# One encoder layer on one core: eight modulation dots moved into the feed-forward's first product, and a block of half 1 summed on chip

## The chip, the cores and the metric

The kernel runs on one core of a Trainium2 chip. The metric is the device time of one execution in microseconds (us), as the median of several executions. One core has a matrix engine (TensorE, PE in the profile; its weight loads are PEld), an elementwise engine (VectorE, DVE), an activation engine (ScalarE, ACT), a general engine (GpSimd, POOL) and an engine that mostly issues DMAs (SyncE, SP). Each runs its own instructions in its own order and waits on semaphores for the others.

## The reference

One layer on x of 1024 positions by 1024 features, in fp32, with one conditioning vector c:

```python
mod = silu(c) @ w_ada + b_ada                 # 6 x 1024 numbers
sh1, sc1, gt1, sh2, sc2, gt2 = split(mod, 6)
h = rmsnorm(x, norm1_g) * (1 + sc1) + sh1
u, v, q, k, va, gate_a, gate_b = split(h @ w_in)
a_out = gmlp_branch(u, v, ...) @ w_a          # spatial gating over chunks of 128
b_out = window_attention_branch(q, k, va, ...) @ w_b
merged = sigmoid(gate_a) * a_out + sigmoid(gate_b) * b_out
x = x + gt1 * (merged @ w_o)
h2 = rmsnorm(x, norm2_g) * (1 + sc2) + sh2
f_gate, f_up = split(h2 @ w_ffn_in)           # 2 x 2816
x = x + gt2 * ((silu(f_gate) * f_up) @ w_ffn_out)
```

## The kernel before

**Products.** Activations lie transposed: features in the 128 partitions, positions along the row. A product of fp32 numbers is made of three products of rounded parts (`mm3`): each operand is split into a high part (a CAST on ACT: `wh`) and the rest (a subtraction on DVE: `wl`), and high times high, high times low and low times high go into one PSUM bank. So every 128 x 1024 unit of weights costs a DMA into a `raw` tile, one CAST on ACT and one subtraction on DVE (a few on POOL) before PE may use it. Nearly all operations are issued through helpers that record every instruction, so almost all rows of the profile carry line 76 (L76); tile names tell them apart.

**Stages.** The 1024 positions are worked in two halves of 512, `hf` 0 and 1. For each half: the QKV products; the attention in eight steps of scores, exponentials, `normalise`, transposes and values, with pieces of other products put in as fillers; the gMLP products; and the branch products `d` = 0..7. In half 1 these are followed by the two sigmoid gates of both halves, by w_o for half 0 (d = 0..7) and for half 1, then by the feed-forward's first product in 22 rows `f` of seven products each (`product(f, i)`, with its evictions in `evict(f, i)`), then by its second product.

**Block products.** The gates and the feed-forward multiply 2 x 2 blocks with seven instead of eight products. The activations' blocks for the gates are made in `block_sums`, from four chunks per k = 0..3: `a0`, `a1` (normalised and scaled x of half 0, from DRAM `x0d`) and `b0`, `b1` (half 1, from DRAM `x1sd`, loaded by POOL's DMA queue in `block_load`). From them come B11, B21 (half 0 plus the shift SH1), T1 to T4 (differences and sums; b1 - b0, b0 - a0, and so on) and B22, which is half 1's second block plus shift, and which is there already as the two tiles `h` (high and low) of half 1's QKV input. `block_part` writes a block's high part by ACT and returns a function that writes the low part by DVE. The eight calls (k, part) are `jobs` at the branch steps d = 2k + part.

**Modulation dots (adaLN).** The first 16 columns of `mod` (SH1, SC1) are made at the start. The other 32 (GT1, SC2, SH2, GT2, eight each) wait in `ada_queue`; each is a dot of a 128 x 1024 tile of weights with `silu_c`, the broadcast silu(c), done by DVE as a multiply with accumulation. They come whole (`ada_load` and `ada_next`), as halves of 128 x 512 in two `hs` or `xs` tiles (`ada_half_load`, `ada_half`), or as pairs loaded by POOL's queue (`ada_pair_load`). Before, five are done in half 0's branch stage, four in half 1's QKV, five in half 1's attention, twelve in the gates, four in w_o of half 0 and two as halves in w_o of half 1. `silu_c` lies in a pool that the feed-forward takes over.

**What sets the order.** A scheduler orders the code of a stage by due times; where `in_order[0]` is set, and in the feed-forward (`tc.manual_schedule()`), the order is that of the code. SP and POOL issue DMAs in order, so a load that waits for a free tile holds up those behind it. `stream("hs")` and `stream("xs")` have two tiles each.

In half 1's attention the dots stand in the step itself, ahead of `normalise`:

```python
            if hf == 1 and 0 < s < 6:
                ada_half("hs" if s < 5 else None)
            elif hf == 1 and s == 0:
                ada_half_load()
            normalise(sc[0], sc[2], den)
```

Of the kernel before, what the change touches and what calls it, by code (L numbers as in the profile page):

```python
# [8 lines left out]
F32 = mybir.dt.float32  # L9
# [3 lines left out]
ALU = mybir.AluOpType  # L13
# [3 lines left out]
P = 128  # L17
# [21 lines left out]
def kernel(  # L39
# [73 lines left out]
    def stream(tag):  # L113
        return t2.tile([P, 512], F32, tag=tag, name=nm(tag), bufs=2)
# [120 lines left out]

    rows_d = lambda n, name, w=HALF: dram.tile([n, P, w], F32, tag=name, name=name)
    x0d, x1sd, pd = rows_d(KT, "x0d"), rows_d(KT, "x1sd"), rows_d(KT, "pd", 2048)
    md = [rows_d(KT, f"md{h}") for h in range(2)]

    apool_ctx = ExitStack()  # L240
# [336 lines left out]
        V.tensor_tensor(s, m[:, :, 0], m[:, :, 1], op=ALU.add)  # L577
        rstd(s, NT, rcol[1])

    dsh = const.tile([P, 16], F32, tag="dsh", name="dsh")[:, :4]  # L580
    blk = {}

    chunk = {}

    def block_load(k, name):
        if k < 4:
            chunk[name] = stream("hs" if name[0] == "a" else "xs")
            store(chunk[name], (x0d if name[0] == "a" else x1sd)[4 * int(name[1]) + k])

# [9 lines left out]
                                              op0=ALU.add, op1=ALU.subtract)  # L599

    def block_sums(k, part, kinds):
        c = slice(k, k + 1)
        a0, a1, b0, b1 = (chunk[x] for x in ("a0", "a1", "b0", "b1"))
        b11 = lambda: block_part("B11", k, a0, kinds[0], mod[:, SH1 + k : SH1 + k + 1])
        b21 = lambda: block_part("B21", k, a1, kinds[0], mod[:, SH1 + 4 + k : SH1 + 5 + k])
        t2 = lambda: block_part("T2", k, b1, kinds[1], mod[:, SH1 + 4 + k : SH1 + 5 + k])
        if k == 3 and part == 0:
            low = b11()
            V.tensor_tensor(b1, b1, b0, op=ALU.subtract)
            low1 = block_part("T3", k, b1, kinds[1], dsh[:, c])  # L610
            low()
            low2 = b21()
            low1()
            low2()
# [3 lines left out]
        if k == 3:  # L618
            V.tensor_tensor(b0, b0, a0, op=ALU.subtract)
            added(b1, a0)  # L620
            low = t2()
            V.tensor_tensor(a1, b1, a1, op=ALU.subtract)
            low1 = block_part("T4", k, a1, kinds[2])
            low()
            low = block_part("T1", k, b0, kinds[1])
            low1()
            low()
            return
        if part == 0:
            if k == 0:  # L630
                V.tensor_tensor(dsh, mod[:, SH1 + 4 : SH1 + 8], mod[:, SH1 : SH1 + 4], op=ALU.subtract)
            V.tensor_tensor(b1, b1, b0, op=ALU.subtract)
            low3 = block_part("T3", k, b1, kinds[1], dsh[:, c])
            V.tensor_tensor(b0, b0, a0, op=ALU.subtract)
            low1 = block_part("T1", k, b0, kinds[1])
            low3()
            added(b1, a0)
            low2 = t2()
            low1()
            low2()  # L640
            block_load(k + 1, "b0")
            for x in blk["B22"]:
                A.activation(x[:, k, :], x[:, k, :].bitcast(F32), AF.Copy, scale=-1.0)
            return
        low, low1 = b11(), b21()
        low()
        low1()
        block_load(k + 1, "a0")
        V.tensor_tensor(a1, b1, a1, op=ALU.subtract)
        low = block_part("T4", k, a1, kinds[2])  # L650
        block_load(k + 1, "b1")
        low()
        block_load(k + 1, "a1")
# [86 lines left out]
    def half(hf):  # L740
# [319 lines left out]
        for s in range(nw):  # L1060
            if s:
                prepare_due()
                sc = q_step(s)
                pts = transposed(st)
                den = exps(*sc, work[s][1])
            fill(FA)
            if hf == 0 and 0 < s < 7:
                x_square(s + 1)
            if hf == 0 and s == 7:
                x_rstd()  # L1070
            if hf == 1 and 0 < s < 6:
                ada_half("hs" if s < 5 else None)
            elif hf == 1 and s == 0:
                ada_half_load()
            normalise(sc[0], sc[2], den)
            if s == 0:
                end_unit()
            st = sc[0]
            if s == nw - 1:
                for vg in vgs:  # L1080
                    act[0] = after(A.activation(vg, vg, AF.Gelu_apprx_tanh), act[0])
                for t, vg in enumerate(vgs[:3]):
                    V.tensor_tensor_reduce(
                        out=stream("hs"), in0=vg, in1=vg, op0=ALU.mult, op1=ALU.add,
                        scale=1.0, scalar=0.0, accum_out=vr[:, t : t + 1])
# [81 lines left out]
        for d in range(KT):  # L1167
            in_order[0] = d < 2
            if 0 < d < KT - 1:
                wab.append(unit(None, V, abr.pop(0)))  # L1170
                if d + 2 + hf < KT:
                    abr.append(raw_unit(w_ab[d + 2 + hf]))
            elif d:
                if hf == 0:
                    early.append(unit(None, V, early_raw[0]))
                else:
                    gate_sums(2)
                    for low in gate_prep_b(2):
                        low()
            if hf and d == 5:  # L1180
                gate_load(2)
            if hf and d == 6:
                gate_prep_a(2)
            ms = []
            for br, t in ((1, (oH, oL)), (0, (gH, gL))):
                if hf and d == KT - 1 and br == 0:
                    held.append((wab[d], t))
                    continue
                pb = mm_bank()
                for k in range(4):  # L1190
                    kc = slice(br * Q + k * P, br * Q + (k + 1) * P)
                    mm3(pb, (wab[d][0][:, kc], wab[d][1][:, kc]), (t[0][:, k, :], t[1][:, k, :]),
                        k == 0, k == 3)
                if d < 2:
                    sg = gates.pop(0)
                    V.scalar_tensor_tensor(out=sg, in0=sg, scalar=1.0, in1=pb, op0=ALU.add,
                                           op1=ALU.mult)
                    ms.append(sg)
                else:
                    c = tmp()  # L1200
                    A.copy(c, pb)
                    j = 2 * hf + br
# [134 lines left out]
    for hf in range(2):  # L1337
# [14 lines left out]
        for d in range(KT):  # L1352
# [34 lines left out]
            if hf == 0:  # L1387
# [17 lines left out]
        sums.append(ss)  # L1405
        if hf == 0:
            m = m1
    assert not ada_queue

    def fpt(name):  # L1410
        return jt(F32R, 4)
# [298 lines left out]
    def split_step(n):  # L1710
        if n < len(work):
# [4 lines left out]
                            for x in "hl"]  # L1716
            split2(raws[n], *ready[n])

    with tc.manual_schedule():
        U[4, 0], U[5, 0], U[0, 0], U[1, 0] = early  # L1720
        buf = mid.tile([P, 2048], F32, tag="mid", name=nm("ws"))
# [44 lines left out]
        for f, i in steps:  # L1766
# [13 lines left out]
                evict(f, i)  # L1780
            if (f, i) == (0, 5):
                evict(0, 6)
            if i == 6 or (f, i) == (0, 5):
                hidden_sums(f)
            elif f > 2:
                run_later(1)
# [174 lines left out]
```

## Time and profile before

| what | value |
|---|---|
| time, median of 3 runs | 1276.61 us (1276.09 to 1276.81) |
| the profiled execution's own time | 1273.99 us |
| its span in the trace | 1272.2 us |
| mean granted TensorE clock | 0.992 |
| busy share of the span | PE 97%, DVE 72%, ACT 45%, POOL 13% |
| DMA | 236.29 MB, mean 186 GB/s |

The span begins with the first and ends with the last instruction of the trace; 1.8 us of the profiled execution's time lie outside it. In the timeline a row gives start, duration, engine, operation, output<-inputs, how many alike follow one another, and in brackets how long the engine stood idle before it and what ended that. In the table of windows each stretch of time has the busy time of every engine with its number of instructions, then the granted clock (PEclk, 1.00 is full), the DMA engines' busy share, and GB/s.

### The profile page before, as it was taken

The page shows a single profiled execution, that of the slowest core. Times are in us where ns is not written, and L with a number is a line of the kernel's source. Part 1 is how long each engine was busy: PE and PEld are TensorE (multiplying, and loading weights), DVE is VectorE, ACT ScalarE, POOL GpSimd, SP SyncE. Part 2 cuts the span into 40 slices and gives each one's busy share as a digit, 9 for nine tenths or more (in the row PEclk, how much of TensorE's full clock was granted, in tenths as well). Part 3 has the DMA queues.
Part 4 walks back from the last instruction along what each step waited for, and adds up shares of the span by engine and source line. Part 5 has one row for each costly group of instructions (what it writes and reads, how often), then busy time and mean ns, then how long its engine had stood idle before and what let it go on. Part 6 is the DMA issues. An engine that isn't in the chain of part 4 may idle for free.

```text
span 1272.2 us, 15652 instructions
## 1 busy us (share of the span) xinstructions
PE 1232.7 (97%) x5634; PEld 1016.3 (80%) x5634; DVE 915.1 (72%) x1545; ACT 577.7 (45%) x938; POOL 170.5 (13%) x216
## 2 busy tenths in 40 slices
PE   6999999999997999999899999999999999999998
PEld 4888887887885788887788888888888887888887
DVE  8898884488887699865888766676666675455646
ACT  5567854366776333443445332333332334433341
POOL 1224320013331001221100000000100000010001
PEclk9999999999999999999999999999999999999999
DMA  9622179313256466677621443554645548896652
GB/s 372 235 100 97 37 240 321 118 55 116 87 177 220 141 215 229 235 245 251 222 110 50 176 171 133 198 185 179 231 150 181 199 165 318 295 329 187 192 167 100
DMA packets 78448, 236.29 MB, mean 186 GB/s; under 512 B 9377, under 2 KB 9377, under 8 KB 72354
## 3 DMA queue, kind: packets, MB, share of 16 engines
q1 hardware_dynamic: 57458, 147.20, 33.9%
q0 software_dynamic: 17456, 81.80, 18.1%
q10 hardware_dynamic: 3456, 6.29, 1.3%
q8 instruction: 44, 0.72, 0.2%
q14 instruction: 34, 0.28, 0.1%
HBM read 178.11 MB, written 57.15 MB: 185 GB/s over the span
## 4 chain that ended last, share of the span: by engine, by line
PE 52%; issue 16%; DVE 12%; DMA 12%; ACT 6%; POOL 1%; SPq 0%; ACTq 0%; POOLq 0%; DVEq 0%
PE at L76 29%; PE mm L76 23%; DVE mid L76 3%; DVE wl L76 2%; ACT wh L76 2%; DMA wo<-in_w_out_dram 1%; DMA raw<-in_w_o_dram 1%; DMA xs<-x1sd 1%; DVE lb L76 1%; DVE xs L76 1%; ACT lb L76 1%; DMA hs<-in_w_ada_dram 1%; DMA wS<-wo 1%; DMA xs<-in_xT_dram 1%; DMA mid<-in_w_ada_dram 1%
## 5 line engine op out<-in xcount | busy, mean ns | idle before, releaser
L76 DVE TENSOR_TENSOR wl<-raw,wh 128x1024 fp32r<-128x1024 f32 x141 | 171.9, 1221 | 94.1 <-ACT wh L76 92.8
L76 ACT CAST wh<-raw 128x1024 fp32r<-128x1024 f32 x155 | 162.4, 1052 | 151.4 <-PE mm L76 51.4
L76 PE MATMUL mm<-mid,wh 128*128 128x512 f32 x696 | 215.5, 390 | 1.6 <-ACT wh L76 1.2
L76 PEld LDWEIGHTS mm<-mid,wh 128*128 128x128 f32 x696 | 130.2, 188 | 30.9 <-ACT wh L76 1.6
L76 PE MATMUL at<-j,wh 128*128 128x512 f32 x464 | 142.9, 389 | 0.0
L76 PE MATMUL mm<-mid,wl 128*128 128x512 f32 x348 | 135.5, 390 | 0.8 <-DVE wl L76 0.6
L76 PE MATMUL mm<-wh,h 128*128 128x512 f32 x384 | 130.9, 403 | 2.2 <-ACT h L76 2.2
L76 PEld LDWEIGHTS at<-j,wh 128*128 128x128 f32 x464 | 87.0, 188 | 18.2 <-ACT xs L76 0.2
L76 PE MATMUL mm<-j,wh 128*128 128x512 f32 x288 | 90.8, 397 | 4.8 <-ACT wh L76 4.8
L76 PE MATMUL at<-h,wh 128*128 128x512 f32 x288 | 91.1, 398 | 3.1 <-ACT h L76 2.8
L76 DVE TENSOR_TENSOR wl<-ws,wh 128x1024 fp32r<-128x1024 f32 (+1 forms) x55 | 62.0, 1128 | 44.4 <-ACT wh L76 44.4
L76 PE MATMUL at<-j,wl 128*128 128x512 f32 x232 | 90.4, 390 | 0.2 <-DVE wl L76 0.2
L76 PEld LDWEIGHTS mm<-wh,h 128*128 128x128 f32 x384 | 72.5, 191 | 17.0 <-ACT h L76 3.1
L76 PE MATMUL mm<-h,wh 128*128 128x512 f32 x272 | 84.6, 392 | 0.0
L76 ACT CAST wh<-ws 128x1024 fp32r<-128x1024 f32 (+1 forms) x55 | 53.6, 974 | 58.8 <-DVE ws L76 42.1
L76 PE MATMUL mm<-wl,h 128*128 128x512 f32 x192 | 77.2, 402 | 2.4 <-DVE wl L76 2.4
L76 PEld LDWEIGHTS mm<-mid,wl 128*128 128x128 f32 x348 | 65.3, 188 | 15.1 <-DVE wl L76 1.0
L76 PEld LDWEIGHTS mm<-j,wh 128*128 128x128 f32 x288 | 54.9, 192 | 16.4 <-ACT wh L76 5.2
L76 PEld LDWEIGHTS at<-h,wh 128*128 128x128 f32 x288 | 54.9, 192 | 15.4 <-ACT h L76 3.2
L76 PEld LDWEIGHTS mm<-h,wh 128*128 128x128 f32 x272 | 50.6, 188 | 10.4
L76 DVE TENSOR_TENSOR ol<-raw,oh 128x1024 fp32r<-128x1024 f32 x30 | 36.7, 1224 | 30.2 <-ACT oh L76 30.0
L76 PE MATMUL mm<-j,wl 128*128 128x512 f32 x144 | 57.5, 399 | 0.9 <-DVE wl L76 0.9
(277 smaller groups left out, 2529.7 us busy)
## 6 DMA issues: line engine op xcount, KB each, us to landing
raw<-in_w_gate_dram SPq DMA_DIRECT2D x28, 512.0 KB, 5.1
tA<-hid POOLq DMA_DIRECT2D x11, 1024.0 KB, 5.2
tB<-hid POOLq DMA_DIRECT2D x11, 1024.0 KB, 4.9
wo<-in_w_out_dram POOLq DMA_DIRECT2D x22, 512.0 KB, 4.8
wS<-wo POOLq DMA_DIRECT2D x11, 1024.0 KB, 5.5
raw<-wS SPq DMA_DIRECT2D x44, 256.0 KB, 3.4
raw<-tB SPq DMA_DIRECT2D x44, 256.0 KB, 4.3
hs<-in_w_ada_dram SPq DMA_DIRECT2D x42, 256.0 KB, 3.6
```

Source lines behind the costliest of these rows:

```text
L76: ins = f(*args, **kw)
```

## The change

Eight dots (GT2) go into the feed-forward: `silu_c` is stored to DRAM near the start, read back into two `hs` tiles at row 6, and rows 7 to 14 do one dot each, in two halves, from weights loaded a row ahead. The five dots of half 1's attention, three of half 0's branch stage, and the two in w_o of half 1 are gone from there; w_o of half 0 does six instead of four, with a third pair load. In the block sums, `b1` is no longer loaded: POOL adds the two parts of B22 (so it has the shift in it), and the biases of T1 to T4 are changed to fit (`nsh` is minus the shift). `gate_sums(2)` moves from d = 7 to d = 6.

```diff
+    silu_d = dram.tile([P, D], F32, tag="silu_d", name="silu_d")
...
     def block_load(k, name):
         if k < 4:
+            if name == "b1":
+                chunk[name] = stream("xs")
+                G.tensor_tensor(chunk[name], *(x[:, k, :].bitcast(F32) for x in blk["B22"]), op=ALU.add)
+                return
...
-        t2 = lambda: block_part("T2", k, b1, kinds[1], mod[:, SH1 + 4 + k : SH1 + 5 + k])
...
+        if part == 0:
+            if k == 0:
+                V.tensor_scalar(nsh, mod[:, SH1 : SH1 + 8], -1.0, None, op0=ALU.mult)
...
             V.tensor_tensor(b1, b1, b0, op=ALU.subtract)
-            low1 = block_part("T3", k, b1, kinds[1], dsh[:, c])
+            low3 = block_part("T3", k, b1, kinds[1], col(nsh, k))
...
+            added(b1, a0)
+            low2 = block_part("T2", k, b1, kinds[1])
...
-        low = block_part("T4", k, a1, kinds[2])
+        low = block_part("T4", k, a1, kinds[2], col(nsh, 4 + k))
...
-            if hf == 1 and 0 < s < 6:
-                ada_half("hs" if s < 5 else None)
-            elif hf == 1 and s == 0:
-                ada_half_load()
+            if hf == 0 and s == 0:
+                store(silu_d, silu_c)
...
-                    gate_sums(2)
...
             if hf and d == 6:
                 gate_prep_a(2)
+                gate_sums(2)
...
-                ada_next(d < 4)
+                ada_next(d < 1)
...
-                if d < 2:
-                    ada_half(None if d else "hs")
...
-                if d in (0, 2):
+                if d in (0, 2, 4):
                     ada_pair_load()
-                if 0 < d < 5:
+                if 0 < d < 7:
                     ada_next(False)
-                if d == 7:
-                    ada_half_load()
...
+    def gain_dots(f, i):
+        if f == EARLY and i == 0:
+            again.extend(stream("hs") for _ in range(2))
+            for j in range(2):
+                dma(again[j], silu_d[:, j * 512 : (j + 1) * 512])
+        if not ada_queue:
+            return
+        if f >= EARLY and i == 5:
+            again[2:] = [tmp(), tmp()]
+            for j in range(2):
+                dma(again[2 + j], w_ada2[ada_queue[0][0] - GT1][:, j * 512 : (j + 1) * 512])
+        if f > EARLY and i in (3, 4):
+            j = int(i == 4)
...
+            V.scalar_tensor_tensor(out=again[2 + j], in0=again[2 + j], scalar=1.0, in1=again[j],
+                                   op0=ALU.mult, op1=ALU.mult,
+                                   accum_out=part if j else acc_mod[:, col : col + 1])
```

PE's order of instructions is the same in both kernels. On the other engines the change moves rows at three places.

On DVE, in a step of half 1's attention, this stands before, between the sink's exponentials (`es`) and the sum of the softmax (`den`) by which `normalise` scales the probabilities `lb`:

```order
L76 TENSOR_TENSOR es_2902<-rows,nmx_2881 128x4
L76 SCALAR_TENSOR_TENSOR hs_2864,acc_mod<-hs_2864,silu_c 128x512
L76 SCALAR_TENSOR_TENSOR hs_2865,part_2949<-hs_2865,silu_c 128x512
L76 TENSOR_TENSOR acc_mod<-acc_mod,part_2949 128x1
L76 SCALAR_TENSOR_TENSOR mod<-acc_mod,badap,cc 128x1
L76 TENSOR_TENSOR den_2931<-den_2931,es_2902 128x4
```

and this after the change, at the same place:

```order
L76 TENSOR_TENSOR es_2888<-rows,nmx_2867 128x4
L76 TENSOR_TENSOR den_2917<-den_2917,es_2888 128x4
L76 RECIPROCAL den_2917<-den_2917 128x4
L76 TENSOR_SCALAR lb_2871<-lb_2871,den_2917 128x384
L76 TENSOR_SCALAR lb_2876<-lb_2876,den_2917 128x384
```

The four rows of a dot are gone, in each of five steps.

On DVE, at the end of half 1's attention and of its gMLP product, `mid_2677<-at,cc,mid_2677` are the evictions of the spatial product and `xs_3802<-xs_3802,xs_3798` is b1 - b0 of the first block sum. Before:

```order
L76 TENSOR_TENSOR xs_3675<-at_3670,xs_3675 64x512
L76 SCALAR_TENSOR_TENSOR mid_2677<-at_3711,cc,mid_2677 128x4x64 x2
L76 SCALAR_TENSOR_TENSOR mid_2677<-at_3720,cc,mid_2677 128x4x64 x2
L76 SCALAR_TENSOR_TENSOR mid_2677<-at_3729,cc,mid_2677 128x4x64 x2
L76 SCALAR_TENSOR_TENSOR mid_2677<-at_3738,cc,mid_2677 128x4x64 x2
L76 TENSOR_TENSOR mid_2681<-at_3761,mid_2680 128x512
L76 TENSOR_TENSOR mid_2681<-at_3768,mid_2680 128x512
L76 TENSOR_TENSOR mid_2681<-at_3775,mid_2680 128x512
L76 TENSOR_TENSOR xs_3802<-xs_3802,xs_3798 128x512
```

After:

```order
L76 TENSOR_TENSOR xs_3620<-at_3615,xs_3620 64x512
L76 TENSOR_TENSOR xs_3747<-xs_3747,xs_3743 128x512
L76 SCALAR_TENSOR_TENSOR mid_2667<-at_3656,cc,mid_2667 128x4x64 x2
L76 SCALAR_TENSOR_TENSOR mid_2667<-at_3665,cc,mid_2667 128x4x64 x2
L76 SCALAR_TENSOR_TENSOR mid_2667<-at_3674,cc,mid_2667 128x4x64 x2
L76 SCALAR_TENSOR_TENSOR mid_2667<-at_3683,cc,mid_2667 128x4x64 x2
L76 TENSOR_TENSOR mid_2671<-at_3706,mid_2670 128x512
```

The subtraction b1 - b0 (now `xs_3747`) stands ahead of the evictions instead of behind them.

On POOL at the same place, `mid<-xs,mid` is the last split of the attention's output and `wl<-raw,wh` a split of weights. Before:

```order
L76 TENSOR_TENSOR mid_2679<-xs_3675,mid_2678 64x4x128
L140 DMA xs_3802<-x1sd 128x512
L76 TENSOR_TENSOR wl_3708<-raw_3705,wh_3707 128x1024
L76 TENSOR_TENSOR wl_3758<-raw_3755,wh_3757 128x1024
L140 DMA hs_3900<-x0d 128x512
```

After:

```order
L140 DMA xs_3743<-x1sd 128x512
L76 TENSOR_TENSOR mid_2669<-xs_3620,mid_2668 64x4x128
L76 TENSOR_TENSOR xs_3747<-h_1927,h_1928 128x512
L76 TENSOR_TENSOR wl_3653<-raw_3650,wh_3652 128x1024
L76 TENSOR_TENSOR wl_3703<-raw_3700,wh_3702 128x1024
```

Where a load was issued, POOL now adds the two parts itself, between the split it has just done and the two splits of weights.

More of the change, by code (lines that the diff above doesn't have):

```diff
@@ L578, in x_rstd @@
         rstd(s, NT, rcol[1])
-    dsh = const.tile([P, 16], F32, tag="dsh", name="dsh")[:, :4]
+    nsh = const.tile([P, 16], F32, tag="nsh", name="nsh")[:, :8]
     blk = {}
@@ L601, in block_sums @@
     def block_sums(k, part, kinds):
-        c = slice(k, k + 1)
         a0, a1, b0, b1 = (chunk[x] for x in ("a0", "a1", "b0", "b1"))
-        b11 = lambda: block_part("B11", k, a0, kinds[0], mod[:, SH1 + k : SH1 + k + 1])
-        b21 = lambda: block_part("B21", k, a1, kinds[0], mod[:, SH1 + 4 + k : SH1 + 5 + k])
-        t2 = lambda: block_part("T2", k, b1, kinds[1], mod[:, SH1 + 4 + k : SH1 + 5 + k])
-        if k == 3 and part == 0:
-            low = b11()
-            V.tensor_tensor(b1, b1, b0, op=ALU.subtract)
-            low1 = block_part("T3", k, b1, kinds[1], dsh[:, c])
-            low()
-            low2 = b21()
+        col = lambda t, i: t[:, i : i + 1]
+        b11 = lambda: block_part("B11", k, a0, kinds[0], col(mod, SH1 + k))
+        b21 = lambda: block_part("B21", k, a1, kinds[0], col(mod, SH1 + 4 + k))
+        if part == 0:
+            if k == 0:
+                V.tensor_scalar(nsh, mod[:, SH1 : SH1 + 8], -1.0, None, op0=ALU.mult)
+            low0 = None
+            if k == 3:
+                low0 = b11()
+            V.tensor_tensor(b1, b1, b0, op=ALU.subtract)
+            low3 = block_part("T3", k, b1, kinds[1], col(nsh, k))
+            if low0:
+                low0()
+                low0 = b21()
+            V.tensor_tensor(b0, b0, a0, op=ALU.subtract)
+            low1 = block_part("T1", k, b0, kinds[1])
+            low3()
+            if low0:
+                low0()
+            added(b1, a0)
+            low2 = block_part("T2", k, b1, kinds[1])
             low1()
+            block_load(k + 1, "b0")
             low2()
@@ L617, in block_sums @@
             return
[L618 to L623, printed above, removed]
+        if k < 3:
+            low = b11()
+            low1 = b21()
             low()
-            low = block_part("T1", k, b0, kinds[1])
+            block_load(k + 1, "a0")
             low1()
[L627 to L648, printed above, removed]
         V.tensor_tensor(a1, b1, a1, op=ALU.subtract)
-        low = block_part("T4", k, a1, kinds[2])
+        low = block_part("T4", k, a1, kinds[2], col(nsh, 4 + k))
         block_load(k + 1, "b1")
@@ L1407 @@
             m = m1
-    assert not ada_queue
+    assert len(ada_queue) == 8
     def fpt(name):
@@ L1717, in split_step @@
             split2(raws[n], *ready[n])
+    again = []
+    def gain_dots(f, i):
[11 more added lines that the diff above has]
+            j = int(i == 4)
+            col = ada_queue[0][0]
+            part = sm(16, "part")[:, :1]
+            V.scalar_tensor_tensor(out=again[2 + j], in0=again[2 + j], scalar=1.0, in1=again[j],
+                                   op0=ALU.mult, op1=ALU.mult,
+                                   accum_out=part if j else acc_mod[:, col : col + 1])
+            if j:
+                added(acc_mod[:, col : col + 1], part)
+                ada_end(col)
+                ada_queue.pop(0)
     with tc.manual_schedule():
@@ L1782 @@
                 evict(0, 6)
+            gain_dots(f, i)
             if i == 6 or (f, i) == (0, 5):
```

## The prediction

> **What bounds the kernel now.** I read the busy shares first, then what PE waited for, then the windows in which those waits lie, and there the timeline.
>
> ```profile
> PE 1232.7 (97%) x5634; PEld 1016.3 (80%) x5634; DVE 915.1 (72%) x1545; ACT 577.7 (45%) x938; POOL 170.5 (13%) x216
> ```
>
> PE is busy 97% of the span, and the change leaves its instructions and their order alone. So only PE's waits can be won, and the time in which it worked at a lower clock. PE's waits by releaser (total us, how often, longest):
>
> ```profile
> PE mm L76 <- ACT wh L76: 6.0, 2, 4.8
> PE mm L76 <- DVE wl L76: 4.3, 6, 2.0
> PE at L76 <- ACT h L76: 2.8, 1, 2.8
> PE at L76 <- DVE xs L76: 2.7, 3, 1.1
> PE at L76 <- POOL rcol L76: 2.4, 1, 2.4
> PE at L76 <- DVE nmx L76: 1.0, 2, 0.8
> ```
>
> These 19.2 us are few and long waits, and they lie in five stretches (windows: length, PE busy, PEld, DVE, ACT, POOL, granted clock, DMA share, GB/s):
>
> ```profile
> 209.00:230.00 21.00, 18.44 (x84) 14.77 (x84) 10.01 (x27) 4.07 (x6) 0.00 (x0) 0.92 0.72 242
> 281.00:340.00 59.00, 55.45 (x282) 45.73 (x281) 50.12 (x155) 39.70 (x98) 19.05 (x11) 0.97 0.29 99
> 398.00:424.00 26.00, 18.78 (x67) 13.80 (x66) 17.22 (x25) 13.88 (x21) 3.23 (x6) 0.87 0.64 198
> 584.00:600.00 16.00, 13.24 (x65) 10.46 (x64) 10.02 (x16) 6.40 (x8) 4.23 (x5) 1.00 0.72 243
> 627.00:645.00 18.00, 14.95 (x59) 12.01 (x58) 11.94 (x16) 8.69 (x12) 1.58 (x2) 0.81 0.47 175
> ```
>
> They are half 1's QKV, half 1's attention, the last block sums with the gates' start, w_o of half 1, and its end. What a stretch can give is PE's idle time plus the share of its busy time that the clock took: 2.56 + 0.08 x 18.44 = 4.0 us in the first, 3.55 + 1.66 = 5.2 in the second, 7.22 + 2.44 = 9.7 in the third, 2.8 in the fourth, 3.05 + 2.84 = 5.9 in the fifth. Together 27.6 us: more than that is hardly to be had. On PE a wait and its aftermath look so:
>
> ```profile
> 223.82 0.58 PE L76 MATMUL mm<-wl,h 128*128 128x512 f32 x1 [2.00 <-DVE wl L76]
> 224.20 0.63 PE L76 MATMUL mm<-wh,h 128*128 128x512 f32 x1
> 224.63 0.63 PE L76 MATMUL mm<-wl,h 128*128 128x512 f32 x1
> 412.03 1.22 PE L76 MATMUL mm<-j,wh 128*128 128x512 f32 x2 [4.78 <-ACT wh L76]
> 597.53 1.16 PE L76 MATMUL at<-ident,rcol 128*128 128x128 f32 x8 [2.39 <-POOL rcol L76]
> 631.98 0.50 PE L76 MATMUL at<-h,wh 128*128 128x512 f32 x1 [2.77 <-ACT h L76]
> ```
>
> After the wait of 2.00 us the matmuls start 0.43 us apart. After the 2.39 us the clock stayed full (1.00 in the window 584 to 600). The Trainium skill's "TensorE: Matmul & The Clock Gate", Part 1, "What's actually happening", has the gate fall to half rate after an idle window of about 3.4 us, which runs freely. By its letter only the wait of 4.78 us would cost clock, and the clock terms of the first, second and fifth stretch (1.5 + 1.7 + 2.8) would not come back with the waits, 6.0 us less to win. The rows above disagree: 0.43 us after a wait of 2.00 us, and 0.81 in the window of the 2.77 us. So the sum goes by the clock column.
>
> **Half 1's QKV.** Its four dots stay, but as other columns, and the queue ahead of them changes. DVE stood still for their loads:
>
> ```profile
> 211.55 0.69 DVE L76 SCALAR_TENSOR_TENSOR hs<-hs,silu_c 128x512 f32<-128x512 f32 x1 [6.92 <-DMA hs<-in_w_ada_dram]
> 221.93 0.69 DVE L76 SCALAR_TENSOR_TENSOR xs<-xs,silu_c 128x512 f32<-128x512 f32 x1 [6.36 <-DMA xs<-in_w_ada_dram]
> ```
>
> The low parts wl wait behind the dots, and PE for wl. Three whole dots with their 512 KB loads on SP leave half 0's branch stage just ahead, so the loads and casts of QKV's weights come earlier. I take the 4.0 us as won; at the least the idle time, 2.6.
>
> **Half 1's attention.** Five dots leave. One step of it on DVE:
>
> ```profile
> 294.00 0.68 DVE L76 SCALAR_TENSOR_TENSOR hs<-hs,silu_c 128x512 f32<-128x512 f32 x1
> ...
> 295.67 0.16 DVE L76 TENSOR_TENSOR den<-den,es 128x4 f32<-128x4 f32 x1
> ...
> 298.27 0.62 PE L76 MATMUL at<-kbuf,mid 128*128 128x384 f32 x2 [1.02 <-DVE xs L76]
> ```
>
> The dot stands 1.67 us ahead of den, and den, lb and xs follow with DVE without a pause; the waits on xs (at most 1.1) and nmx (at most 0.8) are shorter than it. So they go: -5.2, at the least the idle 3.5 us.
>
> **The junction to half 1's branch stage.** Here the change adds a wait.
>
> ```profile
> 356.42 3.23 DVE L76 SCALAR_TENSOR_TENSOR mid<-at,cc,mid 128x256 f32<-128x256 f32 x8 [1.17 <-PE at L76]
> 356.49 1.30 POOL L76 TENSOR_TENSOR mid<-xs,mid 64x512 fp32r<-64x512 f32 x1 [6.14 <-ACT mid L76]
> 358.71 4.74 POOL L76 TENSOR_TENSOR wl<-raw,wh 128x1024 fp32r<-128x1024 f32 x2
> 358.38 2.04 PE L76 MATMUL at<-ident,mid 128*128 128x128 f32 x16
> ```
>
> POOL's add of B22's parts comes behind its split, which ends at 357.8. A 128x1024 subtraction takes POOL 2.37 us, so a 128x512 add about 1.2: done at 359.0. DVE's b1 - b0 (0.69) waits for it and, now standing ahead, holds up the eight evictions, which PE's transposes need: they end at 362.9 instead of 359.65. That is +3.3 us of PE; from +2, if the split comes earlier after a quicker attention, to +4.4, with the next five matmuls 0.2 us slower each.
>
> **Block sums and the gates' start.** DVE waited for b1 from DRAM:
>
> ```profile
> 380.83 0.69 DVE L76 TENSOR_TENSOR xs<-xs,xs 128x512 f32<-128x512 f32 x1 [2.91 <-DMA xs<-x1sd]
> 394.48 0.69 DVE L76 TENSOR_TENSOR xs<-xs,xs 128x512 f32<-128x512 f32 x1 [5.44 <-DMA xs<-x1sd]
> 410.21 0.68 DVE L76 TENSOR_TENSOR raw<-raw,raw 128x512 f32<-128x512 f32 x1
> 410.93 1.04 ACT L76 CAST wh<-raw 128x1024 fp32r<-128x1024 f32 x1
> 413.95 0.79 PE L76 MATMUL mm<-j,wl 128*128 128x512 f32 x1 [0.70 <-DVE wl L76]
> ```
>
> The wait of 4.78 us at 412.03 ends with the cast at 410.93, which follows the weights' sum at 410.21, and that stood in DVE's queue behind k = 3's sums. It now stands ahead of most of them (gate_sums at d = 6), and b1 is there after POOL's 1.2 us. I take the 9.7 us less 1.3 for the wait of 0.70 on wl and one like it: -8.4. DVE and PE are both 3.3 us later from the junction on, so the lead between them stays. At the least 3.0: half of the 4.78, and the other waits left but 0.6.
>
> **The start.** The 0.52 MB store of silu_c runs where DMA is the limit; and a third pair of dots, 1.05 MB, is loaded among w_o's first loads:
>
> ```profile
> 5.00:40.00 35.00, 24.75 (x118) 20.59 (x117) 32.73 (x56) 18.39 (x30) 4.59 (x8) 1.00 0.97 394
> 540.00:545.00 5.00, 5.00 (x24) 4.14 (x23) 3.52 (x5) 2.21 (x3) 1.64 (x3) 1.00 0.95 340
> ```
>
> At 394 GB/s the store is 1.3 us of all DMA engines; PE is idle 10 of 35 us there, for loads. I take +1.0 (0 to 1.3). The Trainium skill's "DMA: Bandwidth & Descriptors", "Issuing engines are not separate DMA queues", has transfers of all issuers share the same engines: by that the store is not free though POOL issues it, and with a share of 0.97 the trace agrees. The pair is 3.1 us at 340 GB/s; PE does not wait in that window, so its lead covers some: +1.3 (0 to 3.1).
>
> **w_o of half 1.** Here the chain is DVE's:
>
> ```profile
> 582.90 0.69 DVE L76 SCALAR_TENSOR_TENSOR hs<-hs,silu_c 128x512 f32<-128x512 f32 x1 [2.23 <-DMA hs<-in_w_ada_dram]
> 584.13 0.75 DVE L76 SCALAR_TENSOR_TENSOR t<-mm,mod,xs 128x512 f32<-128x512 f32 x1
> 595.47 2.01 POOL L76 TENSOR_TENSOR rcol<-ms,nhalf 128x4 f32<-128x4 f32 x1
> ```
>
> A dot waits for its load, the eviction t stands behind it, and SP's next xs and weight loads wait for that eviction: a ring that keeps DVE behind PE until rcol (2.39 us) and h at 631.98 (2.77 us). Both half-dots go, with their loads: -2.8 (1.0 to 2.8) and, for the end, -5.4 (2.0 to 5.9), since about 0.5 of the short waits may stay. The two dots that join half 0 come from POOL's pair, ahead of this.
>
> **The feed-forward's eight dots.** One row of seven products:
>
> ```profile
> 813.00:832.00 19.00, 19.00 (x85) 15.76 (x84) 11.72 (x18) 6.49 (x9) 0.79 (x2) 1.00 0.31 111
> 821.43 0.33 SPq L1427 DMA_DIRECT2D ru<-in_w_up_dram  x1
> hs<-in_w_ada_dram SPq DMA_DIRECT2D x42, 256.0 KB, 3.6
> ```
>
> DVE is idle 7.3 of 19.0 us, and a dot in halves is about 1.9. Its load is issued at product 5, behind the row's last weight load (821.43), and used after product 3 of the next row, five products or 13.6 us later, against 3.6 us of landing. I take 0 (0 to +2).
>
> **The sum.** -4.0 -5.2 +3.3 -8.4 +1.0 +1.3 -2.8 -5.4 +0 = -20.2 us. With every bound at its best, -25.6 (junction +2, nothing for start, pair and feed-forward); at its worst, 1.3 - 2.6 - 3.5 + 4.4 - 3.0 + 3.1 - 1.0 - 2.0 + 2.0 = -1.3. The profiled execution took 1273.99 us and its span 1272.2, so the sum makes 1253.8 there; the median of the runs, 1276.61, is 2.6 higher, so I forecast 1256.4.
>
> **The rivals.** *The block sums stay late.* The wait at 412.03 then ends on k = 3's T sums, whose chunks a0, a1 and b0 still come from DRAM, and the 8.4 us stay: 1264.8. For it: after the change the sums need the same DVE operations, and DVE has now the junction's wait ahead of them. Against it: the longest waits of DVE there name x1sd.
> *Other waits take the place of the removed ones.* If DVE is not what ends last in the four other stretches and only a third of their 17.4 us is won, 1268.0. For it: ACT's wh and h are released last in two of them. Against it: both follow DVE or loads that DVE held up.
> *Slower: the feed-forward's dots stop PE.* Each dot sits in DVE's queue ahead of the next eviction and of low parts of weights. If a dot waits for its load, because SP's queue before it waits for a free tile, that puts a wait like the one at 223.82 into each of eight rows: 2.0 us and six matmuls at 0.43 us instead of 0.22 (85 in 19.00 us), 3.3 us. 8 x 3.3 = 26.4, so 1282.8. It decides from a load that lands over 13.6 us after product 5. Against it: the share of DMA is 0.31 and the lead four times the landing.
> *The costs eat the gains.* All terms at their worst give -1.3, 1275.3. That the change does not do what it says can only be so for the number of dots, which is still 32: DVE works as much as before, elsewhere.
>
> **How the numbers follow.** The forecast gets 0.59, the late block sums 0.17, the replaced waits 0.10, costs that eat the gains 0.03, the feed-forward's stalls 0.11. About 0.2% (2.6 us) is what a measurement of this kernel tells from no change. The first three are faster, 0.86; same 0.03; slower 0.11. The forecast's own range is 1251 (the best bounds) to 1263. The range of 1249 to 1268 adds the first rival and half the second, and 2 us below: PE is idle 1272.2 - 1232.7 = 39.5 us in the span, of which 19.1 lie in the five stretches and 10.3 in the start's window, and a fifth of the other 10 may go too.
>
> **What would show it.** Right: no PE wait on xs and nmx in half 1's attention, none on rcol and none of over 1 us on h near the end of w_o; a new PE wait of about 3 us where the gMLP's transposes begin, on DVE; the wait before the gates' second block row under 2 us. Wrong: PE idle within rows 7 to 14 of the feed-forward, DVE rows there that wait for in_w_ada, or a clock below 1.00 in them.

## The result and the profile after

The changed kernel takes 1265.42 us (median of 13 runs, 1261.93 to 1268.37), the kernel before 1271.87 us (13 runs, 1268.54 to 1276.81). The ratio is 0.9943, 95% interval 0.9926 to 0.9959: 7.3 us faster (5.2 to 9.4); the medians themselves differ by 6.5. The forecast was 20.2 us faster. The three runs of the kernel before that the prediction started from are among the 13 and lie at their upper end; without them the median before would be 1271.05 us, and the medians would differ by 5.6.

The profiled execution took 1264.82 us, 9.2 less than the one before. That one, with 1273.99 us, was 2.1 slower than the median of its kernel. Its busy shares (page, part 1):

```profile
PE 1226.5 (97%) x5634; PEld 1013.4 (80%) x5634; DVE 917.3 (73%) x1548; ACT 577.7 (46%) x938; POOL 176.7 (14%) x218
```

PE's waits by releaser (total us, how often, longest):

```profile
PE at L76 <- DVE mid L76: 5.1, 3, 4.0
PE mm L76 <- DVE wl L76: 3.7, 4, 1.6
PE at L76 <- ACT h L76: 2.8, 1, 2.8
PE at L76 <- DVE rcol L76: 2.0, 1, 2.0
PE mm L76 <- ACT wh L76: 0.9, 1, 0.9
PE at L76 <- DVE xs L76: 0.8, 1, 0.8
PE at L76 <- DVE nmx L76: 0.6, 2, 0.3
```

The wait on POOL's rcol is gone (the 2.0 us on DVE rcol lie at 18.66 us, in the start, where the kernel before waited 0.8), and that on ACT wh fell from 6.0 to 0.9 us. The wait on ACT h is exactly as before, 2.8 us, and a new one of 4.0 us on DVE mid has come. The windows that answer to the five of before, with the junction (345 to 360) as a sixth (length, PE busy, PEld, DVE, ACT, POOL, granted clock, DMA share, GB/s):

```profile
209.00:230.00 21.00, 20.62 (x105) 17.24 (x105) 10.44 (x27) 4.70 (x6) 0.00 (x0) 1.00 0.71 227
281.00:340.00 59.00, 58.72 (x309) 49.76 (x308) 47.63 (x135) 45.53 (x111) 22.22 (x14) 1.00 0.15 50
345.00:360.00 15.00, 10.95 (x62) 9.88 (x61) 10.57 (x16) 10.50 (x18) 7.66 (x4) 0.89 0.33 107
398.00:424.00 26.00, 23.62 (x95) 18.38 (x94) 14.57 (x20) 11.19 (x17) 1.07 (x2) 0.93 0.50 170
575.00:592.00 17.00, 17.00 (x84) 14.34 (x83) 8.92 (x12) 6.93 (x8) 2.72 (x4) 1.00 0.83 288
615.00:632.00 17.00, 13.96 (x55) 10.83 (x54) 11.69 (x17) 8.18 (x11) 1.58 (x2) 0.80 0.51 192
```

Half 1's QKV and attention and the start of w_o of half 1 have no idle time of PE left to speak of. The junction has 4.05 us of it, and w_o's end still has 3.04 at a clock of 0.80.

Since PE runs the same instructions in the same order, each one's start can be set against its start before. How the lead grew and shrank (each stretch begins where the one above it ends):

| stretch | PE's instruction before, after (us) | lead there | change | forecast |
|---|---|---|---|---|
| start | 44.99, 46.61 | -1.62 | +1.6 | +1.0 |
| half 1's QKV | 226.76, 224.81 | 1.95 | -3.6 | -4.0 |
| half 1's attention | 328.78, 320.23 | 8.55 | -6.6 | -5.2 |
| junction | 359.93, 356.79 | 3.14 | +5.4 | +3.3 |
| block sums, gates' start | 415.40, 404.72 | 10.68 | -7.5 | -8.4 |
| gates and w_o of half 0 | 576.19, 567.48 | 8.71 | +2.0 | +1.3 |
| w_o of half 1, start | 597.53, 585.44 | 12.09 | -3.4 | -2.8 |
| w_o of half 1, end | 640.23, 628.27 | 11.96 | +0.1 | -5.4 |
| feed-forward to the end | the last instruction | 9.61 | +2.4 | 0 |

The table sets one execution against one. The runs below give each stretch again, from one profiled execution each, and two rows are not borne out as gains of the change: half 1's QKV, and the block sums with their 7.5 us.

### The profile page after: what moved, and what is told of

Its sections match the earlier page's. It is cut to its first block, busy times and chain, and to the rows that moved or that the text cites. A ratio compares the mean times of both kernels' runs of the same rounds, so it can differ in the third digit from the quotient of the medians.

```text
span 1263.0 us, 15661 instructions
## 1 busy us (share of the span) xinstructions
PE 1226.5 (97%) x5634; PEld 1013.4 (80%) x5634; DVE 917.3 (73%) x1548; ACT 577.7 (46%) x938; POOL 176.7 (14%) x218
## 4 chain that ended last, share of the span: by engine, by line
PE 58%; issue 16%; DVE 13%; DMA 8%; ACT 4%; POOL 1%; SPq 0%; ACTq 0%; POOLq 0%; DVEq 0%
PE mm L76 31%; PE at L76 27%; DVE mid L76 4%; DVE wl L76 3%; DMA hs<-in_w_ada_dram 2%; DMA wS<-wo 2%; DMA wo<-in_w_out_dram 1%; ACT wh L76 1%; DVE hs L76 1%; DVE xs L76 1%; DMA mid<-in_w_ada_dram 1%; DMA hs<-x1d 1%; DVE t L76 1%; DVE ws L76 1%; ACT lb L76 1%
## 5 line engine op out<-in xcount | busy, mean ns | idle before, releaser
L76 ACT ACTIVATE xs<-xs 128x512 f32<-128x512 f32 x21 | 13.3, 633 | 105.3 <-DVE xs L76 105.3
```

The lines of the kernel that those rows point to most:

```text
L76: ins = f(*args, **kw)
```

## The experiments

**The two halves of the change apart.** The first run takes the new block sums out again, the second has them alone:

```diff
-            if name == "b1":
-                chunk[name] = stream("xs")
-                G.tensor_tensor(chunk[name], *(x[:, k, :].bitcast(F32) for x in blk["B22"]), op=ALU.add)
-                return
...
```

The rest of the edit puts back the old biases and order of the sums, and `gate_sums(2)` at d = 7.

> The changed kernel with its block sums as before (b1 loaded from x1sd, dsh, gate_sums(2) at d = 7): the moved dots alone. Theory A (the gains come from the dots, and the block sums' gain is nearly eaten by the junction): against the kernel before, QKV -3.6, attention -6.3, w_o's start -3.0, silu store +1.6, feed-forward and gates up to +2, so about -9 us, and no new wait where the gMLP's transposes begin. Rival B (the block sums carry the gain, since the dots' places fill up): -2 to -4 us. By A the wait of about 5 us before the gates' second block row is still there, by B too.

> The kernel before with the new block sums alone (b1 added by POOL, nsh, gate_sums(2) at d = 6); all dots where they were. Theory A: the junction's new wait of 4 to 5 us eats most of the 7 us won before the gates' second block row: -1 to -3 us. Rival B: -5 to -7 us, because in the kernel before DVE is late at the junction anyway.

The dots alone: 1266.19 us, ratio to before 0.9952 (0.9933 to 0.9970), so 6.1 us faster. The sums alone: 1271.79 us, ratio 0.9999 (0.9980 to 1.0018). Within the noise, the moved dots bring the measured gain and the sums bring nothing by themselves. The first run lies between its theory A (9 us) and its rival (2 to 4). Its trace had won 10.0 us by the end of w_o, but lost 4.4 in the feed-forward, where theory A had up to 2 for the gates and the feed-forward together. Its wait at the junction is gone, and that before the gates' second block row still 4.39 us, which both theories expected. The second run excludes its rival (5 to 7 us); theory A's 1 to 3 us lie partly inside its interval. PE's long waits with the sums alone:

```profile
358.46 3.65 PE L76 MATMUL at<-ident,mid 128*128 128x128 f32 x16 [4.06 <-DVE mid L76]
410.93 1.08 PE L76 MATMUL mm<-j,wh 128*128 128x512 f32 x2 [2.42 <-ACT wh L76]
```

The wait before the gates' second block row shrinks from 4.78 to 2.42 us, and the junction's new wait of 4.06 us takes more than that.

This run also tests half 1's QKV, since its dots stand where they stood before:

```profile
221.85 0.50 PE L76 MATMUL mm<-wl,h 128*128 128x512 f32 x1 [0.49 <-DVE wl L76]
209.00:230.00 21.00, 20.51 (x106) 17.21 (x106) 10.79 (x28) 4.14 (x6) 0.00 (x0) 1.00 0.69 209
```

At the instruction where PE waited 2.00 us in the kernel before, it waits 0.49 here, at full clock. In the stretch of QKV of the table this trace wins 3.5 us, the changed kernel's 3.6. In half 1's attention it wins 0.9 against 6.6, and at the start of w_o of half 1 0.5 against 3.4. So the gains of the last two come from the moved dots. For QKV's this is not shown: the wait of 2.00 us can be one of the execution that was profiled, and how often other executions of the kernel before have it, no trace shows.

**The junction.** On DVE, POOL and PE of the changed kernel:

```profile
350.12 2.82 DVE L76 TENSOR_TENSOR xs<-xs,xs 128x512 f32<-128x512 f32 x1 [3.50 <-POOL xs L76]
352.97 3.23 DVE L76 SCALAR_TENSOR_TENSOR mid<-at,cc,mid 128x256 f32<-128x256 f32 x8
348.79 1.30 POOL L76 TENSOR_TENSOR xs<-h,h 128x512 f32<-128x512 f32 x1
350.04 2.35 POOL L76 TENSOR_TENSOR wl<-raw,wh 128x1024 fp32r<-128x1024 f32 x1
352.34 2.82 POOL L76 TENSOR_TENSOR wl<-raw,wh 128x1024 fp32r<-128x1024 f32 x1
353.99 3.45 PE L76 MATMUL at<-ident,mid 128*128 128x128 f32 x16 [4.05 <-DVE mid L76]
```

DVE waits 3.50 us for POOL's add, as forecast. But then b1 - b0 takes 2.82 us, and it ends at 352.94, 0.55 us after the first of POOL's two splits (352.39). After PE's wait its 16 transposes take 3.45 us instead of 2.04. The same instruction was already slow in the kernel before, where it stood behind the evictions and beside POOL's second split (361.04 to 363.45):

```profile
362.63 1.37 DVE L76 TENSOR_TENSOR xs<-xs,xs 128x512 f32<-128x512 f32 x1
```

The next run puts b1 - b0 behind the evictions (`gm_last[0]` is the last of them):

```diff
-            V.tensor_tensor(b1, b1, b0, op=ALU.subtract)
+            sub = V.tensor_tensor(b1, b1, b0, op=ALU.subtract)
+            if k == 0:
+                after(sub, gm_last[0])
```

> The changed kernel with the first block sum's b1 - b0 put behind the eight gMLP evictions on DVE (an ordering, nothing else). Theory A (this one instruction, waiting for POOL, holds up the evictions and so PE's transposes): PE's wait of 4.05 us on DVE mid goes, with about 1 us of lower clock behind it: -4 to -5 us against the changed kernel. Rival: POOL's add also delays the weight split wl that the next products need, so PE waits there instead and -1 us or less is won.

1262.96 us, ratio to before 0.9916 (0.9891 to 0.9942). In the traces PE's transposes start 4.2 us earlier in relation to the changed kernel and the lead over it is 5.0 us behind them, so the mechanism is shown; but the median is only 2.5 us lower, not the 4 to 5 of theory A. By 402.62 us the lead over the changed kernel has fallen to 2.1 us, here (ACT, then PE):

```profile
396.94 0.72 ACT L76 ACTIVATE mid<-hs,mod 128x512 fp32r<-128x512 f32 x1 [1.32 <-DMA hs<-x0d]
398.61 1.03 ACT L76 CAST wh<-raw 128x1024 fp32r<-128x1024 f32 x1
399.69 1.22 PE L76 MATMUL mm<-j,wh 128*128 128x512 f32 x2 [3.38 <-ACT wh L76]
```

The gates' weights stand in ACT's queue behind a modulation that waits for a chunk from DRAM. In the changed kernel PE came there later and waited 0.88 us; now it waits 3.38. But 0.88 is the luck of one execution: in the four runs below whose code is the changed kernel's up to this instruction, or differs from it only by a later store, PE waits 2.35 to 2.42 us here. In the run with the earlier modulations:

```profile
402.31 0.73 PE L76 MATMUL mm<-j,wh 128*128 128x512 f32 x2 [2.35 <-ACT wh L76]
```

Those four won 3.4 to 5.6 us in the stretch of the block sums, not 7.5, so a part of this give-back is only the difference from a lucky trace.

That POOL makes DVE stand still was tested by giving POOL's two splits at the junction to DVE:

```diff
-        prepare()
+        prepare(V if hf else G)
```

> The changed kernel with the two weight splits wl at the junction done by DVE instead of POOL; in its order b1 - b0 then stands behind the evictions, as in the run with the late subtraction. Theory A (a DVE instruction with two inputs in SBUF stands still while POOL runs one of its own): b1 - b0 takes 0.69 us, where it took 2.82 in the changed kernel and 1.97 in the run with the late subtraction, with POOL's splits beside it. Rival (it is slow for its own operands or their bank, the chunks xs): 2 us or more here too.

b1 - b0 without and with POOL's splits beside it (without, where POOL's last instruction ends at 351.3; then the run with the late subtraction; in both it stands behind the evictions):

```profile
357.64 0.68 DVE L76 TENSOR_TENSOR xs<-xs,xs 128x512 f32<-128x512 f32 x1
```

```profile
351.18 1.97 DVE L76 TENSOR_TENSOR xs<-xs,xs 128x512 f32<-128x512 f32 x1
350.23 5.21 POOL L76 TENSOR_TENSOR wl<-raw,wh 128x1024 fp32r<-128x1024 f32 x2
```

0.68 us against 1.97: theory A. The rival's operands and shapes are the same in both. The time of its one run is 1263.87 us, which says little.

**The end of w_o in half 1.** In the changed kernel, on DVE and PE:

```profile
616.83 0.75 DVE L76 SCALAR_TENSOR_TENSOR mid<-mm,mod,xs 128x512 f32<-128x512 f32 x1
618.33 0.69 DVE L76 TENSOR_TENSOR ss<-ss,t 128x512 f32<-128x512 f32 x1 [0.76 <-ACT t L76]
618.94 0.74 DVE L76 SCALAR_TENSOR_TENSOR mid<-hs,mod,at 128x512 f32<-128x512 f32 x1
620.49 1.58 PE L76 MATMUL at<-h,wh 128*128 128x512 f32 x2 [2.79 <-ACT h L76]
```

The last modulation for the feed-forward (618.94) stands behind the last eviction (616.83) and its sum of squares (618.33). None of them is or follows a dot.

```diff
-                for i in {3: (0, 1), 4: (2,), 5: (3, 4), 6: (5,), 7: (6,)}.get(d, ()):
+                for i in {3: (0, 1, 2), 4: (3,), 5: (4, 5), 6: (6,), 7: (7,)}.get(d, ()):
                     mod2(i)
...
-                mod2(d)
```

> The changed kernel with the modulations of half 0 for the feed-forward (mod2) one step of w_o earlier for features 2, 3, 5, 6, 7, and the last one ahead of the last eviction instead of behind it. Theory A (the wait of 2.8 us on ACT h at w_o's end comes from the chain of the last two modulations behind evictions and sums of squares on DVE, not from the half-dots that left): the wait goes, -3 to -5 us against the changed kernel. Rival (it comes from the x1d and weight loads that share the DMA engines there): the same wait stands at the same place, within 1 us.

1261.73 us, ratio to before 0.9917 (0.9896 to 0.9938), 3.7 us below the changed kernel's median. At the same instruction PE now starts without a wait:

```profile
619.20 0.39 PE L76 MATMUL at<-h,wl 128*128 128x512 f32 x1
619.43 0.62 PE L76 MATMUL at<-h,wh 128*128 128x512 f32 x2
```

In the stretch from 597.53 to 640.23 us of the kernel before, this trace wins 5.4 us, where the changed kernel's lost 0.1. Theory A holds.

**The feed-forward.** Two runs leave out the dots with their loads, or the loads alone (the dot then multiplies silu_c with itself):

```diff
+        if f == EARLY and i == 0:
+            V.memset(mod[:, GT2 : GT2 + 8], 0.0)
+            ada_queue.clear()
+        return
```

```diff
-            for j in range(2):
-                dma(again[2 + j], w_ada2[ada_queue[0][0] - GT1][:, j * 512 : (j + 1) * 512])
...
-            V.scalar_tensor_tensor(out=again[2 + j], in0=again[2 + j], scalar=1.0, in1=again[j],
+            V.scalar_tensor_tensor(out=again[2 + j], in0=again[j], scalar=1.0, in1=again[j],
```

> The changed kernel without the feed-forward's eight dots and their loads; it leaves out GT2 (set to zero), so the output's second part is missing. Theory A (the dots cost 1.5 to 2 us there: a dot stands in DVE's queue between an eviction and the low part of weights that PE waits for, and its loads share the DMA engines): PE's waits on wl and xs within the rows fall from 2.4 us to about 1, and the time by 1.5 to 2 us. Rival B (the two waits come from hid, which waits for the store of wS, with or without dots): the same waits, the time within 1 us of the changed kernel.

> The changed kernel with the feed-forward's eight dots but without their eight loads of weights: each dot multiplies silu_c with itself, so GT2 is another vector. Theory A (of the 2 us that the dots cost, the part in the row with the wait on wl comes from the loads, through the store of wS landing later, and the part on xs from the dot's place in DVE's queue): the wait on wl falls by about 1 us as without dots, that on xs stays at 0.8. Rival (both come from the instructions on DVE): both waits stay as in the changed kernel.

1262.75 us without dots (ratio 0.9912, 0.9885 to 0.9940) and 1264.27 without loads (0.9939, 0.9916 to 0.9961), which is not told from the changed kernel's. PE's waits on wl and xs from 640 us on, in the changed kernel:

```profile
PE mm L76 <- DVE wl L76: 1.6, 1, 1.6
PE at L76 <- DVE xs L76: 0.8, 1, 0.8
PE at L76 <- DVE wl L76: 0.7, 1, 0.7
```

Without dots:

```profile
PE at L76 <- DVE wl L76: 0.7, 1, 0.7
PE mm L76 <- DVE wl L76: 0.4, 1, 0.4
```

With dots and without loads:

```profile
PE at L76 <- DVE xs L76: 0.8, 1, 0.8
PE at L76 <- DVE wl L76: 0.7, 1, 0.7
```

The wait on xs is the dot instruction, that on wl comes with the loads. On DVE of the changed kernel:

```profile
776.75 0.69 DVE L76 TENSOR_TENSOR hid<-hid 128x512 f32<-128x512 f32 x1 [3.81 <-DMA wS<-wo]
777.36 1.22 DVE L76 TENSOR_TENSOR wl<-raw,wh 128x1024 fp32r<-128x1024 f32 x1
778.63 0.50 PE L76 MATMUL mm<-h,wl 128*128 128x512 f32 x1 [1.65 <-DVE wl L76]
...
889.92 0.69 DVE L76 SCALAR_TENSOR_TENSOR t<-t,hs 128x512 f32<-128x512 f32 x1
```

No dot waits for its own load. A sum (hid) waits for the store of wS, whose buffer it writes, and the weights' low part stands behind it. That store is issued (769.09) 1.1 us after the first load of a dot, and the sum can start 7.7 us after the issue; without the loads it is 5.8 us, without dots 7.1. In the seven other traces with dots and loads the store takes 7.2 to 9.0 us to land, in the four without the loads 5.7 to 7.0. So the dots cost about 2 us in this trace, in two of eight rows, at full clock. In the other seven the feed-forward loses 2.4 to 4.8 us against the kernel before: the wait on wl is 1.2 to 3.1 us there, and in four of them about 1.6 us of half clock follow it.

**The store of silu_c.**

```diff
-                store(silu_d, silu_c)
+                after(nc.gpsimd.dma_start(silu_d, silu_c), act[0])
```

> The changed kernel with the store of silu_c put behind the first attention step's exponentials in POOL's order, out of the first 40 us. Theory A (the store costs 1.0 to 1.6 us at the start, because DMA is the limit there): PE is 1 to 1.6 us earlier at 50 us and keeps it. Rival (the first products' waits differ from run to run by as much; the store is 1.3 us of DMA that mostly falls behind the loads PE waits for): within 0.5 us of the changed kernel.

In the trace PE is 1.3 us earlier at 45 us and keeps it to the gates; the time, 1265.08 us (ratio 0.9956, 0.9936 to 0.9976), is not told from the changed kernel's. The traces are with theory A: the eight with the store in the first 40 us lose 1.0 to 3.0 us by 44.99 us of the kernel before, the three without it at most 0.3. The times do not settle it.

**Together.** The late subtraction, the earlier modulations, and gate_prep_b at d = 6 instead of d = 7:

```diff
                 gate_prep_a(2)
                 gate_sums(2)
+                for low in gate_prep_b(2):
+                    low()
```

> The changed kernel with b1 - b0 behind the evictions, the modulations for the feed-forward one step earlier, and the cast and split of the gates' second unit (gate_prep_b) at d = 6, right behind gate_sums(2). Theory A: the junction's 5 us and w_o's end of 4 to 5 us are won, and the 2.9 us that the first gave back at the gates' second block row (a cast that waits in ACT's queue behind a modulation that waits for x0d) is mostly won too: -9 to -11 us against the changed kernel, about 1255 us. Rival (the second block row is bound by the block sums themselves, DVE being busy 90% of that stretch): the give-back stays, -6 to -7 us.

1253.31 us, ratio to before 0.9845 (0.9816 to 0.9873): 19.7 us faster than before, 12.1 below the changed kernel. The give-back of the late subtraction is won too. What is late next, at 397.93, is one low part of B11 in DVE's queue:

```profile
397.93 0.80 PE L76 MATMUL mm<-mid,wh 128*128 128x512 f32 x1 [2.64 <-DVE mid L76]
```

The last run puts it ahead of the weights' sums, and has the late store too:

```diff
                 gate_prep_a(2)
+                block_part("B11", 3, chunk["a0"], kinds[0], mod[:, SH1 + 3 : SH1 + 4])()
                 gate_sums(2)
```

> The combination before, with two things more: the store of silu_c out of the first 40 us, and the low part of B11 for k = 3 ahead of gate_sums(2) in DVE's order. Theory A (the combination's wait of 2.6 us on DVE mid at the gates' second block row is that one low part behind four weight sums in DVE's queue): the wait falls under 1 us and the time by 2 to 4 us against the combination, of which up to 1 from the store. Rival (DVE is full there, and the next thing in its queue comes late instead, T3's or T1's low part or the split wl): within 1 us of the combination.

1252.01 us, ratio 0.9839 (0.9814 to 0.9864). That wait is gone from the trace (2.8 us of lead won there), but 1.6 us come back within the next 10 us in waits on wl, DVE's next rows, and on ACT xs; the 1.3 us between the two combinations lie within their spread. Its median is the lowest of all, but it is not told apart from the first combination's.

## Why the prediction was wrong

The direction and the places of most waits were right, the size was not. The prediction said 20.2 us; on its own base, execution against execution, 9.6 came at PE's last instruction (9.2 in the execution's time), and over the 13 runs of each kernel 7.3.

**Half 1's attention and w_o's start** were right, with 10.0 us in place of 8.0. The attention gave 6.6 instead of 5.2: the window's idle time and clock left out the slower restarts after each wait.

**Half 1's QKV** came out by its number, 3.6 of 4.0, and this is luck. The prediction took a wait that one execution had for a wait of the kernel, and the loads of the dots for its cause. The run with the sums alone has the dots in place and not the wait; and DVE still stands 7.32 and 6.50 us for the loads of dots in the changed kernel (6.92 and 6.36 before), with PE waiting 0.38 us. So 3.6 of the trace's 9.6 us are not shown to come from the change.

**The end of w_o** is the step that failed: "a ring that keeps DVE behind PE until rcol (2.39 us) and h at 631.98 (2.77 us)". It is true for rcol only. That PE waits twice in one stage on late vectors was taken for one cause; the second wait has a chain of its own, which the modulation experiment took away and the leaving dots did not touch (2.77 us before, 2.79 after). The rows of DVE just ahead of 631.98 show it; the prediction quoted none:

```profile
628.04 0.74 DVE L76 SCALAR_TENSOR_TENSOR mid<-mm,mod,xs 128x512 f32<-128x512 f32 x1
629.82 0.69 DVE L76 TENSOR_TENSOR ss<-ss,t 128x512 f32<-128x512 f32 x1 [1.03 <-ACT t L76]
630.43 0.74 DVE L76 SCALAR_TENSOR_TENSOR mid<-hs,mod,at 128x512 f32<-128x512 f32 x1
```

The last modulation (630.43) stands behind the eviction and the sum of squares, as after the change, with no dot in DVE's queue from 598 us on. This is 5.5 us of the 10.6 missing.

**The junction** had the mechanism, the place and the three rows right. The term was mis-sized, +3.3 for 5.4: b1 - b0 was put at 0.69 us, from later rows, and takes 2.82 beside POOL's split (+2.1). In the trace before, this very row already took 1.37. The upper bound of 4.4 allowed for slower matmuls only.

**The block sums' stage** gave 7.5 of 8.4 in this trace, but 3.4 to 5.6 in the four others that have the same code up to there, or a later store: the term was put 3 to 5 us too high. The sums alone measured nothing, and in that run too the wait on wh kept 2.42 us; "under 2 us" held in the changed kernel's own trace alone. "So the lead between them stays" was too kind: the cast of the gates' weights hangs on x0d chunks in ACT's queue, so each us won ahead of it is partly given back there. The rival of the late block sums described this in part.

**The feed-forward** was put at 0 with a bound of +2: 2.4 in this trace, where the run without dots confirms about 2, and up to 4.8 in others. Right that the dots' loads come in time. Overlooked were their neighbours: a store that lands later beside them, and one eviction behind a dot. The rival of stalls in all eight rows was wrong: no dot waits for in_w_ada. Of the prediction's signs of being wrong, PE idle in rows 7 to 14 did come, and in other traces the lower clock behind it.

**Start and w_o of half 0.** +1.6 for +1.0, and +2.0 for +1.3; of the latter, 0.9 us is a wait on DVE mid at 496 us that several of the other runs do not have, so it is not put down to the pair load; the run with the sums alone, without the third pair, loses 1.5 us in this stretch, so no cost of the pair is shown.

## What to carry to other kernels

When several waits of an engine seem to share a cause, follow each one's own queue back from the instruction that ended it before adding it to the sum. A wait that one trace shows is not yet a wait of the kernel: it has to be found in a second execution before it is counted. An instruction that changes engines is priced on both: on its new engine, and for what it stands ahead of on the engine that waits for it. A gain counts only up to the next thing that is late: here the 4.2 us won at the junction met a wait of 3.38 us within 50 us, and only three small reorderings together brought (19.7 us) what had been forecast for the change alone.

## What the runs showed of the hardware

A subtraction on DVE with both inputs in SBUF took 2.82, 1.97 and 1.37 us while POOL ran a subtraction, 0.68 without it, and in all three slow cases ended about 0.55 us after POOL's instruction. The evictions from PSUM beside the same POOL instructions took 0.40 us each (eight in 3.23), as ever. The Trainium skill, "SBUF — State Buffer", section "SBUF: two separate sides", has such DVE instructions and POOL lock one pair of ports for a whole instruction, the loser waiting; the traces agree, and the prediction had not weighed it. It holds the other way too: POOL's later adds of the same shape took 2.14 us instead of 1.30 with DVE busy:

```profile
368.43 2.14 POOL L76 TENSOR_TENSOR xs<-h,h 128x512 f32<-128x512 f32 x1 [2.07 <-DVE hs L76]
```

The lower clock does not follow from a wait's length alone. In the twelve traces it comes in whole stretches of 3.41 us, one to three in a row, and within an execution these stretches lie on one grid of 3.41 us. What tells is how long PE stood idle within one stretch of that grid. The same instruction of the feed-forward waited 2.05 us in the run with the earlier modulations and 2.38 us in the second combination. Its stretches of the grid, in the first and in the second (the grid of the second is taken from its last stretch at half clock):

```profile
772.24:775.65 3.41, 1.36 (x7) 0.81 (x6) 2.46 (x4) 0.00 (x0) 0.00 (x0) 1.00 0.31 129
775.65:779.07 3.42, 3.42 (x10) 2.66 (x9) 2.20 (x3) 1.68 (x2) 0.00 (x0) 0.50 0.00 0
```

```profile
758.86:762.28 3.42, 2.26 (x10) 1.53 (x9) 0.66 (x2) 0.00 (x0) 0.00 (x0) 1.00 0.81 332
762.28:765.69 3.41, 2.19 (x9) 1.80 (x10) 3.06 (x5) 0.84 (x2) 0.00 (x0) 1.00 0.02 10
765.69:769.10 3.41, 3.41 (x16) 2.82 (x15) 2.54 (x4) 1.33 (x2) 0.00 (x0) 1.00 0.00 0
```

The wait of 2.05 us lay in one stretch, and the next had half the clock. The longer one was divided by the grid into 1.16 and 1.22 us, and the clock stayed full. From 40 us to 5 us before the end, every full-clock stretch of the twelve traces with 1.97 us or more of idle PE was followed by half the clock, none with 1.65 or less; between 1.71 and 1.91 both happened. So after the same wait an execution may lose 1.6 us or nothing, by where the grid lies.
